# A two-layer streaming encoder on one core: attention of each chunk worked between the dense products of the next, and the group map folded into the input weights

## The chip, the core and the metric

The kernel runs on one core of one Trainium2 chip. TensorE (PE in the profile, PEld for its weight loads) multiplies, VectorE (DVE), ScalarE (ACT) and GpSimd (POOL) do the elementwise work, and SyncE (SP) issues nearly all transfers; ACT issues a few. The metric is the device time of one execution in microseconds (us), as the median of several runs.

## The reference

Two layers over a sequence of 2048 tokens of 1024 channels. Everything is float32; the kernel splits each operand into a high part of reduced precision (fp32r) and the remainder, and works a product as three matmuls (high by high, high by low, low by high).

```python
# layer 0
h = rms_norm(x, a_norm)
u, z = split(h @ a_w_in)                       # 1024 -> 1024 + 1024
# four groups of 256 channels, windows 2, 4, 8, 16
pooled = trailing_mean(u, window_of_group) - u  # in time, per channel
mixed = einsum('bsgc,gcd->bsgd', pooled, a_w_group) * a_scale
x = x + (mixed * silu(z)) @ a_w_out
x = x + (p[0] @ ple_w[0]) * sigmoid(x @ ple_gate_w[0])
# shared keys and values, 16 heads of 64
k, v = split(rms_norm(x, kv_norm) @ w_kv);  k = rms_norm_per_head(k)
# layer 1
q, z = split(rms_norm(x, b_norm) @ b_w_in); q = rms_norm_per_head(q)
# strictly causal stick-breaking attention:
#   a[t,s] = sigmoid(l[t,s]) * prod_{s<j<t} (1 - sigmoid(l[t,j]))
o = attention(q, k, v)
x = x + (o * silu(z)) @ b_w_out
x = x + (p[1] @ ple_w[1]) * sigmoid(x @ ple_gate_w[1])
```

## The kernel before, in words

The sequence is worked in four chunks of 512 tokens (`NSUB`, `W5`). Activations lie with channels on the partitions, eight tiles of 128x512 to a chunk; weights are the stationary operand, or the moving one where tokens are wanted on the partitions (`run_kvq`).

The program has two parts, one after the other. The first runs, chunk by chunk, a list of 22 steps (`STEPS`): input products u and z by groups of 256 channels (`run_u`, `run_z`), the pooling sums on DVE and POOL, the group map (`run_m`, four matmul blocks to a chunk), output projection (`run_o`), gate (`run_g`), and q, k and v (`run_kvq`). `load_w` brings the weights of the next step while one runs: either raw, to be split by ACT and by DVE or POOL, or ready split from DRAM (`split_once`). The input x and p come with tokens on the partitions and are turned by TensorE transposes against `ident` (L205, L306). What the second part needs goes to DRAM: q, k, v, the split stream (`x2p`), the stream (`x2d`), and split weights for it (`keep`).

The second part is attention from the last chunk to the first. A slot is one head of one query chunk against one key chunk; it has four iterations. An iteration holds a `front` (two matmuls for logits, sigmoid on ACT, the running product as a scan on DVE), a `turn` of an older slot (four transposes, then a copy on ACT and a subtraction on DVE that split the weights) and a `gather` (two matmuls with v). `LAG_T` and `LAG_G` are how many iterations later than its front a turn and a gather stand. Between them a generator (`filler`) yields dense matmuls at a fixed rate: the z products while chunk 3 is in attention (`gate_z`), and the closing products of chunk c+1 (`post`) while chunk c is. The closing products of chunk 0 follow alone at the end, and results are turned by transposes (L765) before they are stored.

Within each engine instructions run in their order; the building layer sets that order by its own estimate of when operands are there. All transfers on SP stand in one queue, and each waits there until its buffer is free.

Of the kernel before, what the change touches and what calls it, by code (L numbers as in the profile page):

```python
# [20 lines left out]
PLE = 256  # L21
W5 = 512
NSUB = S // W5
EPS = 1e-6
WIN = (2, 4, 8, 16)
STEPS = 22
HALO = 16

# [6 lines left out]
def trunk_kernel(ctx, tc, x, p, a_norm, a_w_in, a_w_group, a_scale, a_w_out, kv_norm, w_kv,  # L35
                 k_norm, b_norm, b_w_in, b_q_norm, b_w_out, ple_w, ple_gate_w, out):
# [6 lines left out]

# [3 lines left out]
    V.memset(ones, 1.0)  # L47
    neghalf = cp.tile([P, 8], F32, name="neghalf")
# [10 lines left out]
    r2all = cp.tile([P, NSUB, 4], F32, name="r2all")  # L59
    r2s = [r2all[:, s, :] for s in range(NSUB)]  # L60


    x2d = [[dram.tile([P, W5], F32, name=f"x2d{s}_{o}") for o in range(KT)] for s in range(NSUB)]
    x2p = [[dram.tile([P, 2, W5], F32, name=f"x2p{s}_{o}") for o in range(KT)] for s in range(NSUB - 1)]
    zd = [[dram.tile([P, W5], F32, name=f"zd{s}_{o}") for o in range(KT)] for s in range(NSUB)]
    qd = [[dram.tile([P, 2, W5], F32, name=f"qd{s}_{m}") for m in range(NH // 2)] for s in range(NSUB)]
    kd = [[dram.tile([P, 2, W5], F32, name=f"kd{s}_{m}") for m in range(NH // 2)] for s in range(NSUB)]
    vd = [[dram.tile([8, P, 4, P], F32, name=f"vd{s}_{b}") for b in range(2)] for s in range(NSUB)]
    ve = [[dram.tile([4, W5], F32, name=f"ve{s}_{b}") for b in range(2)] for s in range(NSUB)]

    wod = [dram.tile([P, 2, 2, 4, P], F32, name=f"wod{o}") for o in range(KT)]
    wgd = [dram.tile([P, 2, 2, 4, P], F32, name=f"wgd{o}") for o in range(KT)]
    wzd = [dram.tile([P, 2, 2, 4, P], F32, name=f"wzd{o}") for o in range(KT)]
    wld = [dram.tile([P, 2, 2, P], F32, name=f"wld{o}") for o in range(KT)]

    def rsqrt_mean(out_ap, ss, n, pool, tag):
# [3 lines left out]
        G.tensor_tensor(out=out_ap, in0=ms, in1=neghalf[:, 0:w], op=ALU.pow)  # L80

    state = {"w": 0, "first": True, "deep": False}
    split_once = {}

    def load_w(pools, src, kts, c0, n, gain=None, kept=None):


        wraw, wpair = pools
        units = []
        srcr = src.rearrange("(k q) n -> q k n", q=P)  # L90
        kk = min(W5 // n, kts)
        for k0 in range(0, kts, kk):
            pr = wpair.tile([P, 2, kk, n], F32R, tag="wpair", name="wpair")
            units.append(pr)
            if (kept, c0, k0) in split_once:
                nc.sync.dma_start(out=f(pr), in_=split_once[kept, c0, k0])
                continue
            if state["deep"]:
                raw = io.tile([P, kk, n], F32, tag="io", name="wraw")
            else:  # L100
                raw = wraw.tile([P, kk, n], F32, tag="wraw", name="wraw")
            (nc.scalar if state["first"] else nc.sync).dma_start(out=raw, in_=srcr[:, k0 : k0 + kk, c0 : c0 + n])
            if gain is None:
                A.copy(out=pr[:, 0], in_=raw)  # L104
                state["w"] += 1
                (G if state["w"] % 3 else V).tensor_tensor(out=pr[:, 1], in0=raw, in1=f(pr[:, 0]), op=ALU.subtract)  # L106
            else:
                for j in range(kk):
                    g = gain[:, k0 + j : k0 + j + 1]
                    A.activation(out=pr[:, 0, j], in_=raw[:, j], func=AF.Identity, scale=g)  # L110
                    V.scalar_tensor_tensor(out=pr[:, 1, j], in0=raw[:, j], scalar=g, in1=f(pr[:, 0, j]),  # L111
                                           op0=ALU.mult, op1=ALU.subtract)
            if kept is not None:
                d = split_once[kept, c0, k0] = dram.tile([P, 2, kk, n], F32, name=f"{kept}_{c0}_{k0}")
                nc.sync.dma_start(out=d, in_=f(pr))
        return units

    def wst(units, kt, hl, c0, n=P):
        kk = units[0].shape[2]
        return units[kt // kk][:, hl, kt % kk, c0 : c0 + n]  # L120

    def product(pss_, units, acts, c0s, order=None):

        order = order or range(len(acts))
        for kt in order:
            for ps, c0 in zip(pss_, c0s):
                T.matmul(ps, wst(units, kt, 0, c0), acts[kt][:, 0], start=(kt == order[0]), stop=False)  # L127
                T.matmul(ps, wst(units, kt, 0, c0), acts[kt][:, 1], start=False, stop=False)  # L128
                T.matmul(ps, wst(units, kt, 1, c0), acts[kt][:, 0], start=False, stop=(kt == order[-1]))  # L129
# [748 lines left out]
```

## Time and profile before

| what | value |
|---|---|
| median of 3 runs | 2831.4 us (2830.37 to 2831.97) |
| span of the profiled execution, first to last instruction | 2822.5 us |
| PE busy | 2747.1 us (97%) |
| DVE, ACT, POOL busy | 1892.6, 1409.9, 953.8 us |
| transfers | 576.43 MB, 204 GB/s in the mean |

The profile is of one execution, of which the span is known and no separate time; the median of the runs lies 8.9 us above the span, which is what stands around it (start and end of the execution). Busy time of PE is the union of its matmuls, whose ends are modelled; the mean time of one matmul in the groups is longer than the distance between starts, since matmuls overlap, and the distance is what counts.

### The profile page before, as it was taken

Reading aid. Unit: us, or ns where it says so; the run is one execution under the profiler, and the core shown is the slowest. Engines: PE = TensorE matmul, PEld = TensorE weight load, DVE = VectorE, ACT = ScalarE, POOL = GpSimd, SP = SyncE. Lnnn points to the kernel's source line nnn. Section 1 sums busy time; section 2 is a strip of 40 time slices with the busy share of each in tenths; the row PEclk is TensorE's granted clock in tenths of the full one; section 3 lists DMA queues with packets and bytes.
Section 4 is the critical chain, followed back from the end, with each engine's and each line's share of the span. In section 5 each row is a group of like instructions: output and inputs, shape, how many; then the busy total and the mean of one; then the engine's idle time right before and its main releaser. Section 6 shows DMA issues by size and latency. Waiting matters only on the chain. (4 is left out here: it accounts for less than half of the span.)

```text
span 2822.5 us, 40373 instructions
## 1 busy us (share of the span) xinstructions
PE 2747.1 (97%) x13667; PEld 2271.8 (80%) x13667; DVE 1892.6 (67%) x2581; ACT 1409.9 (50%) x2765; POOL 953.8 (34%) x965
## 2 busy tenths in 40 slices
PE   8999999999999999999899999999999999999999
PEld 6788788888888888888778888887878778878877
DVE  6655534555355543445289999999999998886642
ACT  5445523455244542445356555666666665664431
POOL 3564346643475425644211112121211122223220
PEclk9999999999999999999999999999999999999999
DMA  7855695557855678446666565455555565658765
GB/s 270 274 173 205 238 317 166 175 208 246 303 167 176 221 248 285 147 147 203 213 198 218 185 208 177 161 168 183 171 162 171 168 189 183 195 184 262 242 203 160
DMA packets 335139, 576.43 MB, mean 204 GB/s; under 512 B 32782, under 2 KB 161838, under 8 KB 334932
## 3 DMA queue, kind: packets, MB, share of 16 engines
q1 hardware_dynamic: 327944, 564.34, 60.8%
q10 hardware_dynamic: 6988, 9.50, 1.1%
q8 instruction: 108, 1.77, 0.3%
q14 instruction: 99, 0.81, 0.1%
HBM read 433.16 MB, written 132.19 MB: 200 GB/s over the span
## 5 line engine op out<-in xcount | busy, mean ns | idle before, releaser
L356 PE MATMUL psd<-wpair,x 128*128 128x512 f32 x2304 | 544.0, 393 | 0.0
L630 ACT CAST at<-psa 128x512 fp32r<-128x512 f32 (+3 forms) x640 | 333.4, 522 | 404.8 <-PE psa L627 399.9
L613 DVE TENSOR_TENSOR_SCAN pp<-kap,pp,zeros 128x512 f32<-128x512 f32 x384 | 511.7, 1334 | 5.0 <-ACT kap L606 2.8
L356 PEld LDWEIGHTS psd<-wpair,x 128*128 128x128 f32 x2304 | 428.1, 188 | 86.3
L631 DVE TENSOR_TENSOR at<-psa,at 128x512 fp32r<-128x512 f32 (+3 forms) x640 | 379.7, 595 | 59.2 <-ACT at L630 56.5
L627 PE MATMUL psa<-ident,pp 128*128 128x128 f32 x2176 | 347.4, 275 | 25.0 <-DVE at L631 20.4
L606 ACT ACTIVATE kap<-psl 128x512 f32<-128x512 f32 (+3 forms) x640 | 343.9, 538 | 17.0 <-PE psl L603 8.2
L627 PEld LDWEIGHTS psa<-ident,pp 128*128 128x128 f32 x2176 | 263.3, 140 | 102.8 <-DVE at L631 45.7
L608 POOL TENSOR_SCALAR_AFFINE_SELECT kap<-kap 128x128 f32<-128x128 f32 x256 | 91.7, 359 | 626.8 <-ACT kap L606 532.3
L602 PE MATMUL psl<-kk,qa 128*128 128x512 f32 (+3 forms) x640 | 281.3, 440 | 4.2 <-ACT vr L393 3.5
L613 DVE TENSOR_TENSOR_SCAN pp<-kap,zeros 128x128 f32<-128x128 f32 (+3 forms) x256 | 213.9, 836 | 40.5 <-POOL kap L608 37.0
L640 PE MATMUL pso<-at,vv 128*128 128x512 f32 (+3 forms) x640 | 235.4, 368 | 0.0
L603 PE MATMUL psl<-kk,qb 128*128 128x512 f32 (+3 forms) x640 | 234.6, 367 | 0.0
L639 PE MATMUL pso<-at,vv 128*128 128x512 f32 (+3 forms) x640 | 232.5, 363 | 1.3 <-ACT at L630 1.2
L127 PE MATMUL psd<-xp,wpair 128*128 128x512 f32 x512 | 200.2, 391 | 2.4 <-ACT xp L172 2.4
L111 DVE SCALAR_TENSOR_TENSOR wpair<-wraw,gains,wpair 128x512 fp32r<-128x512 f32 x192 | 149.6, 790 | 78.4 <-ACT wpair L110 78.1
L128 PE MATMUL psd<-xp,wpair 128*128 128x512 f32 x512 | 200.1, 391 | 0.0
L129 PE MATMUL psd<-xp,wpair 128*128 128x512 f32 x512 | 199.8, 390 | 0.0
L110 ACT ACTIVATE wpair<-wraw,gains 128x512 fp32r<-128x512 f32 x192 | 136.8, 720 | 113.2 <-DMA wraw<-in_w_kv_dram 69.2
L106 POOL TENSOR_TENSOR wpair<-wraw,wpair 128x512 fp32r<-128x512 f32 x107 | 146.0, 1369 | 62.1 <-ACT wpair L104 40.7
L104 ACT CAST wpair<-wraw 128x512 fp32r<-128x512 f32 x160 | 97.7, 619 | 114.2 <-PE psd L129 109.1
L639 PEld LDWEIGHTS pso<-at,vv 128*128 128x128 f32 x640 | 120.5, 188 | 28.4 <-ACT at L630 2.6
(204 smaller groups left out, 5488.9 us busy)
## 6 DMA issues: line engine op xcount, KB each, us to landing
wpair<-wi SPq DMA_DIRECT2D x96, 512.0 KB
kk<-kd SPq DMA_DIRECT2D x320, 128.0 KB
vv<-vd SPq DMA_DIRECT2D x160, 256.0 KB
wraw<-in_w_kv_dram SPq DMA_DIRECT2D x128, 256.0 KB
wpair<-wzd SPq DMA_DIRECT2D x64, 512.0 KB
wpair<-wod SPq DMA_DIRECT2D x64, 512.0 KB
wpair<-wgd SPq DMA_DIRECT2D x64, 512.0 KB
wi<-wpair SPq DMA_DIRECT2D x32, 512.0 KB
```

What stands on the lines that cost most here:

```text
L127: T.matmul(ps, wst(units, kt, 0, c0), acts[kt][:, 0], start=(kt == order[0]), stop=False)
L128: T.matmul(ps, wst(units, kt, 0, c0), acts[kt][:, 1], start=False, stop=False)
L356: T.matmul(pss2[i], ck["x2"][kt][:, xh, tk], wst(ws, kt, wh, 0, W5), start=(kt == 0 and xh == 0 and wh == 0), stop=(kt == KT - 1 and wh == 1))
L602: T.matmul(ps[:, :w], qa[:, qs], kk[:, :w], start=True, stop=False)
L603: T.matmul(ps[:, :w], qb[:, qs], kk[:, :w], start=False, stop=True)
L606: A.activation(out=kp[:, r0:], in_=ps[:, :w], func=AF.Sigmoid, scale=-1.0)
L613: V.tensor_tensor_scan(out=pp[:, r0:][:, ::-1], data0=kp[:, r0:][:, ::-1], data1=zeros.to_broadcast([P, w]), initial=1.0 if st["diag"] els ...
L627: T.transpose(pt[:, j * P : (j + 1) * P], pp[:, r0 + kt * P : r0 + (kt + 1) * P], ident)
L630: A.copy(out=at[:, 0, cs], in_=pt[:, cs])
L631: V.tensor_tensor(out=at[:, 1, cs], in0=pt[:, cs], in1=f(at[:, 0, cs]), op=ALU.subtract)
L639: T.matmul(po[:, cs], vv[:, kt, :], at[:, 0, cs], start=(st["diag"] and kt == 0), stop=False)
L640: T.matmul(po[:, cs], vv[:, kt, :], at[:, 1, cs], start=False, stop=(st["last"] and kt == 3))
```

## The change

The whole body is written anew; the operations of attention stay as they were. What is different:

- **Order of the work.** There is one stream of dense work for all chunks (`stream`): the first part of a chunk up to its first eight heads' q, k, v (`first_part`), the other eight heads (`second_part`), and so on to chunk 3, then the closing products of chunks 0 to 2 (`post`). Attention now goes from chunk 0 to chunk 3. Only the first part of chunk 0 and the closing products of chunk 3 stand alone. In between, every iteration of attention on chunk c has the dense products of chunk c+1 (for chunk 3: the closing products) before and after its gather, 1584 dense matmuls to the 64(c+1) iterations of a chunk (`rate`).
- **Group map.** Since the pooling acts on time and the map on channels, `fold` multiplies the u columns of the input weights by the group map once (48 matmuls of 256 columns per group), stores the split product, and `run_m` and its 48 matmuls per chunk are gone. Two of the folds stand ahead of the first dense product, two between those of chunk 0.
- **Layouts.** The host lays x, p and the result out by channels and the weights in the blocks that are loaded, so the transposes of x, p and the result are gone. The squares of x for its norm are summed over channels by POOL and by small matmuls with `ones` (L274).
- **Buffers.** Dense products have two PSUM banks beside attention (six while they stand alone); weights have 9 units of 512 KB (`UNITS`), given back one by one (`give_back`) as the last token tile or channel block has used them; raw weights, x and other inputs share six tiles (`io`). Scans run in place. `LAG_T`, `LAG_G` are 5 and 6, before 6 and 8.
- **Engines.** The pooling adds all run on DVE, the splitting of the chunks' x on POOL; the split of gated outputs moves from ACT and DVE to ACT and POOL, goes to DRAM and comes back. In `keyed`, reduction, root and multiplication of a token tile are issued together; before, they were issued for two tiles at a time.

```diff
+    def pump():
+        while wq["out"] < len(plan) and wq["out"] - wq["back"] < UNITS:
+            ...
+            held.append(unit(key, src, kts, n, gain, keep))
+            wq["out"] += 1
...
+    def fold(g):
+        (wg, _), = take(1)
+        ...
+                raw = io("uraw")
+                nc.sync.dma_start(out=raw, in_=wu_t[2 * g + c, :, h * W5 : (h + 1) * W5])
+                ...
+                    for l, r in ((0, 0), (1, 0), (0, 1)):
+                        T.matmul(ps[:, e], parts[c, kt // 4][l][:, ks], wg[:, r, c],
                                 start=(c == 0 and l == r), stop=(c == 1 and r == 1))
+                        yield
+            ...
+            nc.sync.dma_start(out=d, in_=f(pr))
...
+    def keyed(s, kind, b, j, ps, rj):
+        ...
+        V.tensor_reduce(out=ss, in_=sq.rearrange("q (h d) -> q h d", d=HD), op=ALU.add, axis=AX.X)
+        rsqrt_mean(rq, ss, HD, "q")
+        V.tensor_tensor(out=q8, in0=q8, in1=rq.unsqueeze(2).to_broadcast([P, 8, HD]), op=ALU.mult)
...
+    def first_part(s):
+        yield from mixer(s)
+        x1 = yield from out_steps(ck["m"], lambda o: x[o * P : (o + 1) * P, s * W5 : (s + 1) * W5])
+        ple = load_ple(0, s)
+        yield from gate_steps(x1, ple, put_x2(s))
+        ck["side"] = prep(s + 1) if s + 1 < NSUB else iter(())
+        yield from every(gate_z(s), 48, ck["side"])
+        for kind in "qkv":
+            yield from every(kvq(s, kind, 0), 48, ck["side"])
...
+    def stream():
+        yield from first_part(0)
+        for c in range(NSUB):
+            yield from second_part(c)
+            if c < NSUB - 1:
+                yield from first_part(c + 1)
+        for c in range(NSUB - 1):
+            yield from post(c)
...
+    for n in range(4 * len(slots) + LAG_G):
+        ...
+            turn(active[i2], j2)
+        ...
+            front(active[i], j)
+        fill(x_ / 2)
+        ...
+            gather(active[i3], j3)
+        fill(x_ / 2)
+    for _ in run:
+        pass
+    state["solo"] = True
+    for _ in post(NSUB - 1):
+        pass
```

Three places show how the order moves. The first is PE's row in an iteration of attention. Before, with chunk 3 in attention (`psa` are the transposes, `psl` the logits, `pso` the products with v, `psd` the dense products, here the z products of a chunk read back from DRAM, `xz`):

```order
L627 MATMUL psa<-ident,pp 128x128 x4
L602 MATMUL psl<-kk,qa 128x512
L603 MATMUL psl<-kk,qb 128x512
L668 MATMUL psd<-xz,wpair 128x512
L670 MATMUL psd<-xz,wpair 128x512
L672 MATMUL psd<-xz,wpair 128x512
L639 MATMUL pso<-at,vv 128x128
L640 MATMUL pso<-at,vv 128x128
```

And now, with chunk 1 in attention and the q, k, v products of chunk 2 between (L421; the numbered `x` are the eight tiles of its stream):

```order
L646 MATMUL psa<-ident,pp 128x128 x4
L628 MATMUL psl<-kk,qa 128x512
L629 MATMUL psl<-kk,qb 128x512
L421 MATMUL psd<-wpair,x_11005 128x512 x2
L421 MATMUL psd<-wpair,x_11114 128x512 x3
L421 MATMUL psd<-wpair,x_11214 128x512
L658 MATMUL pso<-at,vv 128x512
L659 MATMUL pso<-at,vv 128x512
L421 MATMUL psd<-wpair,x_11214 128x512 x2
L421 MATMUL psd<-wpair,x_11333 128x512 x3
L421 MATMUL psd<-wpair,x_11418 128x512 x2
```

An iteration holds 13 dense matmuls where it held 3, and they are of the earlier stage, whose weights DVE must split.

The second place is DVE's row in the q and k products. Before, in the first part, between the reduction of squares (L422) and the multiplication by the root (L430), where L111 splits weights, and L173 splits the next chunk's x:

```order
L422 TENSOR_REDUCE ssq<-sqq 128x8
L111 SCALAR_TENSOR_TENSOR wpair<-wraw,gains,wpair 128x512
L422 TENSOR_REDUCE ssq<-sqq 128x8
L430 TENSOR_TENSOR qn<-qs,rq 128x512 x2
L111 SCALAR_TENSOR_TENSOR wpair<-wraw,gains,wpair 128x512 x3
L173 TENSOR_TENSOR xp<-pst,xp 128x512
L422 TENSOR_REDUCE ssq<-sqq 128x8
```

Now, late in the program, with attention's scans (L635) and subtractions (L650) around the same pair (L463, L466) and the splitting of weights (L136):

```order
L463 TENSOR_REDUCE ssq<-sqq 128x8
L466 TENSOR_TENSOR qs<-qs,rq 128x512
L650 TENSOR_TENSOR at<-psa,at 128x512
L635 SCALAR_TENSOR_TENSOR pp<-pp,zeros 128x512
L650 TENSOR_TENSOR at<-psa,at 128x512
L635 SCALAR_TENSOR_TENSOR pp<-pp,zeros 128x128
L650 TENSOR_TENSOR at<-psa,at 128x512
L635 SCALAR_TENSOR_TENSOR pp<-pp,zeros 128x256
L136 SCALAR_TENSOR_TENSOR wpair<-wraw,gains,wpair 128x512
L463 TENSOR_REDUCE ssq<-sqq 128x8
L136 SCALAR_TENSOR_TENSOR wpair<-wraw,gains,wpair 128x512
L466 TENSOR_TENSOR qs<-qs,rq 128x512
```

The multiplication, which needs POOL's root, follows its reduction with nothing or one instruction between, and attention's scans now queue behind it.

The third place is SP's queue at the start. Before, x (`xin`) is loaded at once and the first stores of split weights (`wi`) follow it:

```order
L465 DMA grow<-in_a_norm_dram 8x128
L182 DMA xin<-in_x_dram 128x512 x8
L472 DMA hrow<-in_k_norm_dram 1x64 x2
L465 DMA grow<-in_a_scale_dram 8x128
L465 DMA grow<-in_b_norm_dram 8x128
L465 DMA grow<-in_kv_norm_dram 8x128
L472 DMA hrow<-in_b_q_norm_dram 1x64 x2
L115 DMA wi_0_369<-wpair 128x1024
```

Now the group maps and z weights come first, then three of the eight x tiles, the stores of the split z weights (`once`), and only then the u weights for the folds (`uraw`):

```order
L146 DMA wraw<-in_a_w_group_dram 128x512 x2
L146 DMA wraw<-in_wz_a_dram 128x512 x4
L297 DMA xin<-in_x_dram 128x512 x3
L150 DMA once_336<-wpair 128x1024
L150 DMA once_345<-wpair 128x1024
L150 DMA once_354<-wpair 128x1024
L150 DMA once_363<-wpair 128x1024
L237 DMA uraw<-in_wu_t_dram 128x512 x4
L297 DMA xin<-in_x_dram 128x512 x5
L237 DMA uraw<-in_wu_t_dram 128x512 x4
```

The first matmuls of PE, those of the fold, stand behind the u weights, and the u weights behind four stores that wait for ACT and DVE.

More of the change, by code (lines that the diff above doesn't have):

```diff
@@ L118, in wst @@
[L118 to L129, printed above, removed]
@@ new lines, in mixer @@
+    def mixer(s):
+        ck = chunk[s]
+        ck["m"] = {}
+        for g in (3, 2, 1, 0):
+            us, zs = take(4), []
+            for k in range(2):
+                ps = dense()
+                yield from product(ps, us, ck["x"], k * P, k)
+                zs.append(silu(ps, ck["rb1"]))
+            us = take(4)
+            for k in range(2):
+                ps = dense()
+                yield from product(ps, us, ck["x"], k * P, k)
+                pooled(s, 2 * g + k, ps, zs[k])
+            if s == 0 and g > 1:
+                yield from fold(g - 2)
@@ new lines, in trunk_kernel, with fill @@
+    for _ in fold(3):
+        pass
+    side = prep(0)
+    for _ in range(KT):
+        next(side)
+    for _ in fold(2):
+        pass
+    for _ in side:
+        pass
+    until((0, 0))
+    state["solo"] = False
+    begin(0)
+    begin_v(0)
+    for _ in range(24):
+        next(run)
+    owed = 0.0
+    count = 0
+    def fill(share):
+        nonlocal owed, count
+        owed += share
+        while owed >= 1.0:
+            next(run, None)
+            owed -= 1.0
+            count += 1
+            if count % 36 == 0 and kept:
+                keep(*kept.pop(0))
```

1255 lines of the change are left out of this document (563 added, 692 removed).

## The prediction

> **What bounds the kernel now.** I read the table of engines, then what PE waited for, then busy times by stretches cut where the kind of work changes. PE carries the time:
>
> ```profile
> PE 2747.1 (97%) x13667; PEld 2271.8 (80%) x13667; DVE 1892.6 (67%) x2581; ACT 1409.9 (50%) x2765; POOL 953.8 (34%) x965
> ```
>
> Only 75.4 us of the span are not PE's, so a change gains by taking matmuls away, or by at most those 75. The stretches say where they lie (columns: length, then busy us of each engine, granted clock, DMA share, GB/s):
>
> ```profile
> 0.00:20.00 20.00, 8.32 (x27) 5.79 (x28) 7.10 (x53) 11.69 (x30) 1.02 (x8) 1.00 0.72 252
> 20.00:250.00 230.00, 223.38 (x991) 183.43 (x990) 139.42 (x215) 103.18 (x202) 124.87 (x107) 0.99 0.67 229
> 250.00:1250.00 1000.00, 994.78 (x4549) 823.42 (x4548) 488.23 (x692) 433.29 (x776) 493.54 (x428) 1.00 0.64 217
> ...
> 1380.00:1450.00 70.00, 55.92 (x270) 42.94 (x268) 37.40 (x47) 26.77 (x52) 11.19 (x15) 0.93 0.71 214
> 1450.00:2680.00 1230.00, 1202.85 (x6604) 1000.71 (x6603) 1106.27 (x1404) 735.03 (x1524) 256.72 (x341) 1.00 0.60 190
> 2680.00:2822.50 142.50, 131.90 (x630) 107.88 (x628) 49.29 (x78) 38.80 (x82) 21.16 (x25) 0.97 0.57 182
> ```
>
> PE's idle time is 11.7 us at the start, 6.6 in the rest of chunk 0, 5.2 in 1000 us of dense work (0.5%, DVE 49% busy), 14.1 at the joint between the parts, 27.2 in 1230 us of attention (2.2%, DVE 90% busy) and 10.6 in the last 142. In attention PE waits for DVE:
>
> ```profile
> PE psa L627 <- DVE at L631: 20.4, 40, 1.3
> ```
>
> **The change, part by part.** The distance between starts of dense matmuls, in a run of them and beside attention, and of attention's own (start, duration, line):
>
> ```profile
> 1290.70 20.46 PE L356 MATMUL psd<-wpair,x 128*128 128x512 f32 x89
> 1311.00 1.03 PE L439 MATMUL pst<-ident,qn 128*128 128x128 f32 x8
> ```
>
> ```profile
> 1603.65 0.40 PE L668 MATMUL psd<-xz,wpair 128*128 128x512 f32 x1
> ...
> 1604.35 0.39 PE L639 MATMUL pso<-at,vv 128*128 128x512 f32 x1
> ...
> 1604.81 0.60 PE L627 MATMUL psa<-ident,pp 128*128 128x128 f32 x4
> 1605.16 0.47 PE L602 MATMUL psl<-kk,qa 128*128 128x512 f32 x1
> 1605.47 0.39 PE L603 MATMUL psl<-kk,qb 128*128 128x512 f32 x1
> 1605.70 0.39 PE L668 MATMUL psd<-xz,wpair 128*128 128x512 f32 x1
> ...
> 1615.92 0.28 PE L639 MATMUL pso<-at,vv 128*128 128x256 f32 x1
> 1616.04 0.28 PE L640 MATMUL pso<-at,vv 128*128 128x256 f32 x1
> ```
>
> A dense matmul takes 20.30/89 = 0.228 us in a run and 0.70/3 = 0.233 beside attention; one of 256 columns 0.12; four transposes 0.35, and the matmul behind them comes 0.08 late (0.31 for 0.23), so 0.43. One full iteration of attention is 0.46 (v) + 0.43 + 0.47 = 1.36 us of PE.
>
> 1. The group map's 4 x 48 matmuls go: 192 x 0.228 = -44.
> 2. The folds come: 192 of 256 columns x 0.12 = +23.
> 3. Transposes of x (128), p (64) and the result (128) go, 80 groups of four x 0.43 = -34 (0.35 to 0.45 a group: -28 to -36). Their copies on ACT and DVE lay beside PE and count nothing.
> 4. 16 more one-column matmuls for the norm of x, each at most a transpose's 0.09: +2.
> 5. Dense matmuls beside attention are 6336, before 2064 (z products and three of four closings). At 0 to 0.005 us more each the 4272 cost 0 to 21; the runs between are now 6 to 13 long for the first chunks, so nearer the run: +8.
> 6. The joint goes: attention starts while the stream has more to give. 14.1 us idle, and 0.07 of clock over 70 us (4.9): -14 to -19, I take -16.
>
> 7. **The opening.** Ahead of the last u tile of the first fold SP has issued 5.5 MB, of the second 7.9 MB (0.26 MB a raw tile, 0.52 a split one). At the 252 GB/s of the first 20 us that is 22 and 31 us; the first z product follows the second fold at about 34. By then PE has worked some 12 us, so 22 are lost where 11.7 were: +10. The last folded weights of chunk 0 stand 37.2 MB down the queue, and PE comes to them after 22 + 23 + 7 x 48 x 0.228 = 122 us. What the queue delivers:
>
> ```profile
> 60.00:100.00 40.00, 40.00 (x178) 33.14 (x177) 29.52 (x51) 20.68 (x45) 17.86 (x19) 1.00 0.80 278
> 705.60:776.20 70.60, 70.60 (x317) 58.44 (x316) 26.00 (x41) 16.33 (x31) 33.03 (x36) 1.00 0.88 303
> ```
>
> At 303 GB/s 37.2 MB take 123 us, at 278 134, at 252 148: 1 to 26 us late, of which I take 8. Together +18, between +8 and +36. The Trainium skill (DMA: Bandwidth & Descriptors, Specifications) gives about 358 GB/s to a core; the 303 GB/s at a share of 0.88 agree (344 at a full share), and by the page's figure the queue would be done at 104 us, the 8 would fall away and the sum would be 8 lower.
>
> 8. **Stalls beside attention.** Durations of DVE and of POOL's root (POOL is the second fence):
>
> ```profile
> L613 DVE TENSOR_TENSOR_SCAN pp<-kap,pp,zeros 128x512 f32<-128x512 f32 x384 | 511.7, 1334 | 5.0 <-ACT kap L606 2.8
> L631 DVE TENSOR_TENSOR at<-psa,at 128x512 fp32r<-128x512 f32 (+3 forms) x640 | 379.7, 595 | 59.2 <-ACT at L630 56.5
> L613 DVE TENSOR_TENSOR_SCAN pp<-kap,zeros 128x128 f32<-128x128 f32 (+3 forms) x256 | 213.9, 836 | 40.5 <-POOL kap L608 37.0
> L111 DVE SCALAR_TENSOR_TENSOR wpair<-wraw,gains,wpair 128x512 fp32r<-128x512 f32 x192 | 149.6, 790 | 78.4 <-ACT wpair L110 78.1
> L430 DVE TENSOR_TENSOR qn<-qs,rq 128x512 f32<-128x512 f32 x64 | 49.0, 766 | 42.6 <-POOL rq L80 42.3
> L422 DVE TENSOR_REDUCE ssq<-sqq 128x8 f32<-128x512 f32 x64 | 43.7, 682 | 67.8 <-ACT sqq L420 67.8
> L448 DVE SCALAR_TENSOR_TENSOR hl<-pst,gqk,hl 128x512 fp32r<-128x512 f32 x32 | 23.1, 744 | 0.0
> ```
>
> ```profile
> L80 POOL TENSOR_TENSOR rq<-ms,neghalf 128x8 f32<-128x8 f32 x64 | 109.3, 1708 | 5.3
> ```
>
> Attention asks DVE for about 1.33 + 0.67 = 2.0 us a full iteration and 1.3 a diagonal one, PE for 1.36 and 0.9. One block of q or k (96 matmuls, 22.1 us of PE) asks DVE for 8 x 0.79 + 4 x 0.68 + 4 x 0.77 + 4 x 0.74 = 15.1. With 11.3 iterations beside it in chunk 2 that is DVE 35 against PE 36 us, with 15.5 in chunk 3 43.5 against 42. Outside q, k and v DVE has a fifth to spare. And the multiplication behind the reduction now waits for POOL's 1.7 us with nothing or one instruction between, with attention's scans queued behind it. Before, that wait was 42.3/64 = 0.7 us and cost PE nothing; now I put it at 1 to 2, four times a block: +5 us, so 40 against 36 in chunk 2 (four blocks) and 49 against 42 in chunk 3 (two). The lag of turn behind front, about one and a half iterations, swallows some 5 us once in each pair, which leaves 8 + 9 = 17 of stall. The rest: 985 us beside chunks 0 and 1 at 0.5%, 5 us, and about 910 beside 2 and 3 at attention's 2.2%, 20. Together 42, of which 27 were there: +15, between -15 and +60.
>
> 9. The end: the same 432 closing matmuls alone; the last turn and its copy (about 1 us) go, the last pair of gated outputs now takes a split on POOL: 0, between -3 and +6.
>
> Sum: -44 + 23 - 34 + 2 + 8 - 16 + 18 + 15 = -28 on the span of 2822.5, 2794.5; with the 8.9 us by which the median stands above the span, 2803. ACT (50%) stays covered, as does the unchanged volume of transfers (about 580 MB).
>
> **The rivals.**
>
> *Nearly no stalls.* Beside attention DVE's load is now even, and PE loses 0.5 to 1% throughout, as it did at 49%: 15 us in place of 42, and the queue of the opening keeps up: 2803 - 27 - 8 = 2768. For it speaks the dense stretch; against it the 90% stretch, whose load the blocks of q and k reach again. Chance 0.23.
>
> *Transfers hold PE in chunk 0.* Opening at 252 GB/s: 18 later than taken. Beside attention on chunk 0, 121 MB in 456 us are 265 GB/s, and the kept weights, stores and k, q, v share one queue; if six blocks wait 2 us each: 2803 + 18 + 12 = 2833. Against it: 303 GB/s went with PE never idle. Chance 0.14.
>
> *DVE becomes the bound (slower).* The place is q, k and v beside chunks 2 and 3. POOL's work, 21% of attention's stretch before, is about 32% beside chunk 2, and the same operation is longer with the other engine at work, on both:
>
> ```profile
> L173 DVE TENSOR_TENSOR x<-ta,x 128x512 fp32r<-128x512 f32 x32 | 32.2, 1007 | 36.5 <-ACT x L172 35.4
> ...
> L173 DVE TENSOR_TENSOR x<-tx,x 128x512 fp32r<-128x512 f32 x32 | 22.2, 693 | 13.4 <-ACT x L172 13.0
> ```
>
> ```profile
> L265 POOL TENSOR_TENSOR zr<-zr,sg 128x512 f32<-128x512 f32 x32 | 42.5, 1350 | 23.7 <-ACT sg L264 20.2 <-DMA wpair<-wi 3.5
> ...
> L712 POOL TENSOR_TENSOR zr<-zr,sgz 128x512 f32<-128x512 f32 x32 | 63.1, 1971 | 174.4 <-issue 83.5 <-DVE os L645 74.0 <-ACT sgz L711 12.0
> ```
>
> If DVE runs 10% longer there, each of the nine blocks is some 4 us over PE, and POOL's late root adds 1 to 2 us at each of 24 tiles: +50, so 2853. It decides from about 7% on, where 22 us are eaten. Beside this stands the Trainium skill (SBUF — State Buffer, the reading of its diagram): DVE with two SBUF inputs and GpSimd share a port pair under an exclusive lock, and the loser blocks for a whole instruction; the pairs of rows above agree in kind. Chance 0.17.
>
> **How the numbers follow.** My sum has 0.46; 2803 is its time, with 2780 to 2822 its own range. The range of all reaches from 2762 to 2856, which leaves a tenth on either side. Within 0.2% (5.7 us, about what a measurement tells from no change) of 2831.4 lies most of the transfers' case: same 0.10. Slower: the DVE case and some of the transfers', 0.20. Faster: 0.70.
>
> **What would show it.** PE's busy time should fall by about 45 us to some 2700; the first dense product start near 34 us; no gap at any change of chunk over 3 us; PE's waits beside chunks 2 and 3 be for DVE's subtraction, densest in q and k, with DVE itself waiting for POOL's root about 1.5 us each. I am wrong if PE's idle time passes 125 us (then look whether DMA or DVE is named), or if PE's busy time does not fall.

## The result, and the profile after

The changed kernel takes 2964.6 us (median, 2961.81 to 2968.24); the kernel before took 2831.2 beside it. The ratio is 1.0473, 95% interval 1.0459 to 1.0488: 133 us slower, where 28 us faster was forecast. The profiled execution has a span of 2960.0 us. Its table of engines:

```profile
PE 2763.0 (93%) x13376; PEld 2260.2 (76%) x13376; DVE 1955.7 (66%) x2513; ACT 1355.7 (46%) x2642; POOL 966.2 (33%) x961
```

PE's idle time went from 75.4 to 197.0 us (+122), and its busy time did not fall by some 45 but rose by 16. What PE waited for (total, times, longest):

```profile
PE pst L475 <- DVE qs L466: 70.8, 16, 9.7
PE psd L248 <- ACT uh L239: 24.4, 4, 19.3
PE pso L659 <- DVE at L650: 20.3, 29, 2.7
PE psd L221 <- ACT mp L117: 9.8, 4, 4.7
```

L475 is the turn of finished rows of q or k (`finish`), the transposes that lay them out by channels. There are 16 groups of rows, and PE waits at every one: at 15 for the multiplication L466 (at one of them twice), at the last for a copy on ACT (5.4 us). L659 is attention's product with v; it waits for DVE's subtraction about as long as attention's transposes did before (20.4). By stretches (columns as in the prediction):

```profile
0.00:140.00 140.00, 113.53 (x569) 96.75 (x570) 88.86 (x190) 61.68 (x123) 48.57 (x48) 0.98 0.82 284
...
320.00:420.00 100.00, 81.39 (x366) 65.59 (x365) 46.45 (x66) 43.95 (x75) 34.46 (x35) 0.93 0.62 196
420.00:800.00 380.00, 350.99 (x1606) 287.05 (x1606) 204.11 (x263) 158.52 (x318) 189.60 (x190) 0.96 0.79 258
800.00:960.00 160.00, 132.97 (x619) 107.29 (x618) 90.36 (x129) 76.99 (x145) 58.13 (x61) 0.91 0.56 175
960.00:1320.00 360.00, 349.75 (x1704) 288.21 (x1702) 245.60 (x296) 160.76 (x328) 147.52 (x147) 0.99 0.60 188
1320.00:1500.00 180.00, 159.45 (x764) 129.83 (x765) 117.02 (x158) 94.91 (x180) 58.66 (x67) 0.94 0.53 166
...
2160.00:2840.00 680.00, 660.64 (x3392) 540.31 (x3391) 541.13 (x637) 323.14 (x643) 110.66 (x123) 0.99 0.67 210
```

The three bad stretches, 320 to 420, 800 to 960 and 1320 to 1500, are where rows of q and k end. There PE loses 66 of 440 us, and the granted clock is 0.91 to 0.94. DVE is busy 46 to 65% of them, so it is not at its limit. Two of the waits end before attention's first matmul (391.2 us); from 320 to 391 us:

```profile
PE pst L475 <- DVE qs L466: 12.9, 2, 7.5
```

Chunk by chunk the waits are 21.4, 23.3, 15.7 and 10.3 us: they are largest where the least attention runs beside the products. One such wait, from the timeline of all engines (start, duration, engine, line; in brackets the idle time ahead and what ended it):

```profile
806.31 0.67 ACT L459 ACTIVATE qs<-psd,r 128x512 f32<-128x512 f32 x1
...
808.76 0.64 PE L421 MATMUL psd<-wpair,x 128*128 128x512 f32 x2
...
810.71 0.62 ACT L117 CAST xp<-xin 128x512 fp32r<-128x512 f32 x1 [2.56 <-DMA xin<-in_x_dram]
...
811.77 0.61 ACT L461 ACTIVATE sqq<-qs 128x512 f32<-128x512 f32 x1
...
812.41 0.69 DVE L463 TENSOR_REDUCE ssq<-sqq 128x8 f32<-128x512 f32 x1 [1.45 <-ACT sqq L461]
812.63 1.27 POOL L288 TENSOR_TENSOR acc<-acc,sq 128x512 f32<-128x512 f32 x1
...
815.48 1.65 POOL L114 TENSOR_TENSOR rq<-ms,neghalf 128x8 f32<-128x8 f32 x1
817.10 1.26 POOL L118 TENSOR_TENSOR xp<-xin,xp 128x512 fp32r<-128x512 f32 x1
817.16 1.74 DVE L466 TENSOR_TENSOR qs<-qs,rq 128x512 f32<-128x512 f32 x1 [1.76 <-POOL rq L114]
819.05 0.45 PE L475 MATMUL pst<-ident,qs 128*128 128x128 f32 x1 [9.66 <-DVE qs L466]
```

The last token tile's row leaves ACT at 807.0. Its square stands on ACT behind a cast of the next chunk's x, which waits 2.56 us for its transfer; its root comes on POOL behind that x's sum of squares; the multiplication takes 1.74 us where it mostly takes 0.69, beside POOL's split of x (five of the 64 take over 1.7 us, and all five stand beside a POOL instruction). PE has long come to the turn, and everything behind the turn waits. The granted clock around it (third column from the right):

```profile
806.00:810.00 4.00, 2.69 (x11) 1.72 (x11) 4.00 (x7) 1.96 (x4) 0.00 (x0) 1.00 0.38 122
810.00:814.00 4.00, 0.00 (x0) 0.00 (x0) 1.65 (x3) 2.66 (x5) 2.59 (x3) 0.80 0.96 259
814.00:818.00 4.00, 0.00 (x0) 0.00 (x0) 2.06 (x2) 0.00 (x0) 3.83 (x4) 0.50 0.61 164
818.00:822.00 4.00, 2.95 (x10) 2.51 (x11) 2.11 (x3) 1.38 (x2) 0.36 (x1) 0.50 0.04 15
822.00:826.00 4.00, 4.00 (x22) 3.28 (x20) 1.26 (x3) 2.21 (x6) 0.94 (x1) 0.92 0.98 332
```

It falls to half some 3 us into the wait and is still at half 3 us after its end. So a wait costs twice: its own time, and slow matmuls behind it. Over the span the mean clock is 0.975, before 0.996; (1 - clock) x span is 74 and 11 us. Part of that lies in idle time, so it bounds the slow matmuls from above.

The line in the code that made this is not among those that the prediction weighed. In `run_kvq`, now `kvq`, finished rows are turned later, beside products of the next block:

```diff
-                    while j0 == 0 and kt == KT - 1 and lag:     # behind 48 matmuls
+                if kt in (2, 5) and j < 2 and lag:              # the first behind 9 matmuls
                     lag.pop(0)()
```

48 matmuls are 11 us of PE, 9 are 2 us (and a little more with attention between). The chain from a product's end to its finished row takes 5.3 us where nothing stands between (from 313.11 to 318.36, six instructions on ACT, DVE and POOL), and 12.6 in the wait above (806.31 to 818.90).

### The profile page after: what moved, and what is told of

It is laid out like the page before. It is cut to its first block, busy times and chain, and to the rows that moved or that the text cites. A ratio compares the mean times of both kernels' runs of the same rounds, so it can differ in the third digit from the quotient of the medians.

```text
span 2960.0 us, 39525 instructions
## 1 busy us (share of the span) xinstructions
PE 2763.0 (93%) x13376; PEld 2260.2 (76%) x13376; DVE 1955.7 (66%) x2513; ACT 1355.7 (46%) x2642; POOL 966.2 (33%) x961
## 5 line engine op out<-in xcount | busy, mean ns | idle before, releaser
L635 DVE TENSOR_TENSOR_SCAN pp<-pp,zeros 128x512 f32<-128x512 f32 (+3 forms) x640 | 779.2, 1219 | 119.5 <-POOL pp L633 91.4
L421 PE MATMUL psd<-wpair,x 128*128 128x512 f32 x2304 | 623.9, 408 | 2.2 <-DVE wpair L136 1.4
L650 DVE TENSOR_TENSOR at<-psa,at 128x512 fp32r<-128x512 f32 (+3 forms) x640 | 384.9, 603 | 320.1 <-ACT at L649 318.2
L421 PEld LDWEIGHTS psd<-wpair,x 128*128 128x128 f32 x2304 | 437.0, 196 | 89.7 <-DVE wpair L136 4.1
L646 PEld LDWEIGHTS psa<-ident,pp 128*128 128x128 f32 x2176 | 278.4, 142 | 94.4 <-DVE pp L635 8.3
L631 ACT ACTIVATE pp<-psl 128x512 f32<-128x512 f32 (+3 forms) x640 | 343.6, 538 | 10.2 <-PE psl L629 7.2
L221 PE MATMUL psd<-x,wpair 128*128 128x512 f32 x768 | 304.7, 397 | 9.7 <-ACT sg L397 6.1
L223 PE MATMUL psd<-x,wpair 128*128 128x512 f32 x768 | 303.7, 395 | 0.2 <-DVE x L118 0.2
L226 PE MATMUL psd<-x,wpair 128*128 128x512 f32 x768 | 302.9, 394 | 0.0
L633 POOL TENSOR_SCALAR_AFFINE_SELECT pp<-pp 128x128 f32<-128x128 f32 x256 | 89.5, 350 | 554.4 <-ACT pp L631 553.8
L659 PE MATMUL pso<-at,vv 128*128 128x512 f32 (+3 forms) x640 | 239.9, 375 | 20.8 <-DVE at L650 20.3
L136 DVE SCALAR_TENSOR_TENSOR wpair<-wraw,gains,wpair 128x512 fp32r<-128x512 f32 (+1 forms) x224 | 165.9, 782 | 35.0 <-ACT wpair L135 34.5
L221 PEld LDWEIGHTS psd<-x,wpair 128*128 128x128 f32 x768 | 145.7, 190 | 40.4 <-ACT sg L397 7.5
L135 ACT ACTIVATE wpair<-wraw,gains 128x512 fp32r<-128x512 f32 (+1 forms) x224 | 145.7, 688 | 57.4 <-DMA wraw<-in_w_kv_dram 16.9
```

Source lines behind the costliest of these rows:

```text
L221: T.matmul(ps, hi, acts[kt][:, 0], start=(i == 0), stop=False)
L223: T.matmul(ps, hi, acts[kt][:, 1], start=False, stop=False)
L226: T.matmul(ps, lo, acts[kt][:, 0], start=False, stop=(i == n))
L421: T.matmul(ps, ck["x2"][kt][:, xh, tk], u[:, wh, 0], start=(kt == 0 and xh == wh), stop=(kt == KT - 1 and wh == 1))
L631: A.activation(out=pp[:, r0:], in_=ps[:, :w], func=AF.Sigmoid, scale=-1.0)
L635: V.tensor_tensor_scan(out=pp[:, r0:][:, ::-1], data0=pp[:, r0:][:, ::-1], data1=zeros.to_broadcast([P, w]), initial=1.0 if st["diag"] els ...
```

## The experiments

Two theories. *Position*: PE waits because the turn now stands nearer to its rows than their chain is long. *Load*: DVE or POOL (the prediction's rival) have too much to do beside attention, and the turn is only where it shows. All runs, against runs of the kernel before on the same chip; "turn" is PE's wait at the turn for DVE's multiplication:

| kernel | median us | ratio to before [95%] | PE idle | turn | clock |
|---|---|---|---|---|---|
| before | 2828.5 to 2831.2 | 1 | 75.4 | 0 | 0.996 |
| changed | 2964.6 | 1.0473 [1.0459, 1.0488] | 197.0 | 70.8 | 0.975 |
| e3_before_early | 2930.7 | 1.0360 [1.0345, 1.0375] | 137.2 | 68.2 | 0.979 |
| e10_before_early_fill | 2948.4 | 1.0419 [1.0403, 1.0434] | 114.9 | 43.0 | 0.989 |
| e2_warm | 2986.3 | 1.0561 [1.0543, 1.0579] | 169.1 | 50.6 | 0.982 |
| e11_no_row_norm | 2849.9 | 1.0074 [1.0057, 1.0091] | 123.3 | 0 | 0.988 |
| e1_late_turn | 2921.8 | 1.0332 [1.0308, 1.0357] | 167.9 | 44.7 | 0.983 |
| e5_side_off | 2958.3 | 1.0453 [1.0435, 1.0470] | 195.2 | 67.4 | 0.976 |
| e6_late_turn_side_off | 2903.8 | 1.0254 [1.0239, 1.0269] | 156.7 | 30.1 | 0.984 |
| e7_side_in_gate | 2922.1 | 1.0325 [1.0310, 1.0341] | 165.7 | 24.6 | 0.981 |
| e9_cover33 | 2904.0 | 1.0263 [1.0245, 1.0280] | 160.3 | 9.5 | 0.987 |
| e4_u_first | 2970.0 | 1.0497 [1.0482, 1.0513] | 207.9 | 74.2 | 0.972 |
| b1_before_layouts | 2842.0 | 1.0042 [1.0027, 1.0056] | 112.3 | | 0.986 |
| b2_norm_later | 2835.5 | 1.0022 [1.0012, 1.0032] | 99.0 | | 0.988 |
| b4_norm_dve | 2834.8 | 1.0018 [1.0009, 1.0027] | 107.8 | | 0.991 |
| b3_p_out | 2808.6 | 0.9926 [0.9912, 0.9940] | 78.0 | | 0.995 |

**Position alone: the turn moved in the kernel before.**

```diff
-                    while j0 == 0 and kt == KT - 1 and lag:
+                    while j0 == 0 and kt == 1 and lag:
```

> The kernel before, with the turn of a finished group of q or k rows moved ahead: 12 dense matmuls behind the end of its last token tile, where it stood 48 behind. There is no attention beside these products. Theory 'position alone makes the stall': 16 waits of some 3 to 6 us, with the clock falling behind them; 2831 rises by 60 to 120 us. Rival 'only the load of attention makes the chain of that tile long': less than 40 us.

Measured +102 us, with no attention beside these products. PE's waits:

```profile
PE pst L439 <- DVE qn L430: 68.2, 32, 3.9
```

Idle time rose by 62 us and PE's busy time by 41 (2747.1 to 2788.1), though PE does the same work: position is enough, and a microsecond of waiting costs some 0.65 more in clock. The clock behind one of these waits (2.43 us, ended at 1391.23):

```profile
1388.00:1391.00 3.00, 0.80 (x4) 0.33 (x2) 2.31 (x4) 1.40 (x3) 2.29 (x3) 1.00 0.35 100
1391.00:1394.00 3.00, 1.59 (x5) 0.88 (x5) 0.87 (x2) 0.00 (x0) 1.87 (x2) 0.52 0.24 80
1394.00:1397.00 3.00, 3.00 (x11) 2.41 (x11) 1.50 (x2) 1.38 (x2) 0.00 (x0) 0.50 0.15 61
1397.00:1400.00 3.00, 3.00 (x17) 2.66 (x16) 1.04 (x2) 1.38 (x2) 0.00 (x0) 0.85 0.72 288
```

**The chain left out.** In `keyed` of the changed kernel the square, reduction, root and multiplication are gone, so the rows stay unnormed; the turn stays where it is.

> The changed kernel without the norm of the rows of q and k: squares, reduction, root and multiplication of all 64 token tiles are left out, the turn stands where it stood. Theory 'chain and position': the turn then waits for one ACT operation alone, the 70.8 us of waits fall under 12 and the clock comes back: 2850 to 2880 us, no lower than the kernels with the late turn would reach if their turns waited for nothing. Rival 'DVE's and POOL's load is the bound, the turn only shows it': with 92 us of DVE and 109 us of POOL gone, the waits for DVE's subtraction in attention (20.3 us) fall too, and the time goes under 2835.

Measured 2849.9, at the lower edge of what position forecast. The table of engines, and PE's waits in attention and at the turn:

```profile
PE 2727.7 (96%) x13376; PEld 2240.8 (79%) x13376; DVE 1868.9 (66%) x2385; ACT 1320.6 (46%) x2578; POOL 836.7 (29%) x833
```

```profile
PE pso L652 <- DVE at L643: 19.5, 26, 3.2
...
PE pst L468 <- ACT qs L459: 5.5, 6, 1.3
```

DVE has 87 us less and POOL 129, and PE still waits 19.5 us for DVE in attention (L652 here is L659 of the changed kernel). This run takes away the chain and some of the load together, so it can't part the two by its time alone. But the load that went did not shorten the waits in attention, and with all releasers counted PE's waits at the turn fell from 83.3 to 8.3 us, which is the whole of the 74 us of idle time that went. Of the span, 109 us went (2960.0 to 2851.0): these 74, and 35 of PE's busy time. In medians it is 115 us, the price of the chain at this place; it is most of what the changed kernel lost, and without it the kernel is still 0.74% slower than before.

**Cover against length.** Four edits of the changed kernel: the turn later (e1), the next chunk's x in the middle of tiles (e5), both (e6), both with still more cover (e9).

```diff
-                if kt in (2, 5) and j < 2 and lag:
+                if (j, kt) in ((0, 7), (1, 1), (1, 4), (1, 6)) and lag:      # e1, e6, e7
+                if (j, kt) in ((1, 2), (1, 4), (1, 5), (1, 7)) and lag:      # e9
```

```diff
-            if i % n == 0:       # in every(): a step of the next chunk's x
+            if i % n == 12:      # e5, e6, e9
```

> The changed kernel with one thing moved: the turn of a finished group of q or k rows stands at least 21 dense matmuls (some 5 us) behind the end of its last token tile, where it stood 9 (2 us) behind. Theory 'position': PE waits for the chain of that tile (ACT, DVE, POOL, DVE), so the waits of PE's row transposes for DVE's multiplication (16 waits, 70.8 us) fall under 15 us, and the clock beside them comes back (75 us were lost to it in the span, 11 before the change); time falls from 2965 to some 2850 to 2880 us. Rival 'load': DVE, ACT and POOL are behind by their load, so the waits move to other places with the same sum; time falls by less than 20 us.

> The changed kernel with the steps that bring in and split the next chunk's x (ACT and POOL) moved by 12 matmuls: in a block of q, k or v they stood behind the 48th and the 96th matmul, that is right behind the ends of the second and the last token tile, and now behind the 12th and the 60th, in the middle of tiles. Theory 'the chain of the last tile waits on ACT and POOL behind that step': the 16 waits of the row transposes fall from 70.8 to 25 to 40 us, and the time from 2965 by 30 to 60 us. Rival 'the chain is long by itself and the turn stands too near': the waits stay over 60 us, the time within 10 us.

> Both edits: the turn 21 matmuls behind the end of the last token tile, and the steps of the next chunk's x in the middle of tiles. If cover and length of the chain together make the wait, the waits of the row transposes fall under 10 us (44.7 with the late turn alone) and the clock lost beside them goes too: 2860 to 2890 us. If a third thing holds the chain (the weights' split on ACT, which waits there for raw weights), 20 us or more of waits stay and the time is 2900 or more.

> As the kernel with the late turn and the x steps in the middle of tiles, but the first turn stands 33 dense matmuls (7.5 us) behind the end of the last token tile, where it stood 24. The chain there took 10.8 us at its longest and the longest wait was 5.9. If the wait is cover against length of chain, 2 us more of cover take the 12 waits (30.1 us) under 12 us, and with the clock behind them the time falls from 2904 to some 2875 to 2890. If the chain stretches with the cover, because the building layer orders ACT and POOL by what is wanted first, it stays within 8 us of 2904.

None reached its first forecast. The late turn gave 43 us, between the numbers of the two theories; the steps of x alone gave 6, as their rival had it; both together gave 61, the second case's number, and ACT did wait there for raw weights (1.93 us ahead of a square at 322.18). With 33 matmuls of cover the wait for the multiplication is down to 9.5 us, as the first case had it, and the time did not move:

```profile
PE pst L475 <- DVE hl L482: 15.2, 7, 3.2
PE pst L475 <- DVE qs L466: 9.5, 6, 4.0
```

The four turns of a group now stand close together (behind matmuls 33, 39, 42 and 48), and they wait for DVE to have read an earlier turn out of one of the two banks (L482). With all releasers counted, the waits at the turn went only from 37.6 (e6) to 32.7 us. More cover helps, but these four edits won only about half of the chain's price (61 us of 115). In the kernel before the four turns stand together behind 48 matmuls, and wait 5.1 us for banks that attention does not share; a place as late as that was not tried in the changed kernel, so whether it would win the rest stays open.

**The steps of x taken out of these blocks altogether** (into the gate products, `every(gate_z(s), 18, ...)`; the turn as in e1):

> The late turn, and all ten steps of the next chunk's x moved out of the q, k and v blocks into the gate products ahead of them. Nothing of the next chunk then stands on ACT, POOL or the transfer queue beside the rows. The waits of the row transposes fall under 10 us as with both edits; if the transfers of x held ACT by holding the raw weights in the queue, this one has fewer waits than the kernel with the steps in the middle of tiles. 2855 to 2890 us. Against it: the gate products then carry ten splits, and waits for ACT's sigmoid there could rise from 6 us by some 10.

```profile
PE pst L475 <- DVE qs L466: 24.6, 12, 3.8
PE psd L248 <- ACT uh L239: 23.9, 3, 19.1
PE pst L274 <- POOL acc L288: 20.0, 3, 10.9
```

Measured 2922.1, which misses the forecast. The turn waits less than in e1, which has it at the same place (24.6 against 44.7), so x does lengthen the chain. But the norm's small matmuls (L274) now stand right behind POOL's sum of squares and wait 20.0 us: the same fault at another place.

**Filling the waits.** 18 useless matmuls ahead of the first turn of each group, in the changed kernel and in the kernel before with the early turn:

```diff
+                if m == 0:
+                    x0 = chunk[s]["x2"][0][:, 0]
+                    for i in range(18):
+                        T.matmul(pt.rearrange("q j t -> q (j t)"), x0[:, 0:P], x0, start=True, stop=True)
```

> The changed kernel with 18 useless 512-column matmuls ahead of the first transposes of each of the 16 finished groups of rows, written to the bank that the transposes then overwrite: 16 x 18 x 0.228 = 66 us more of PE work, which stands where PE otherwise waits. Theory 'idle time costs twice, since the granted clock falls behind a wait of several us': PE's idle time falls by some 45 us or more, the mean clock rises, and the time falls by 20 to 45 us though PE does more work. Rival 'the clock falls for other reasons than the waits': the time stays or rises by up to 20 us.

> The kernel before with the early turn, and 18 useless 512-column matmuls (4.1 us) ahead of each of its 16 first turns, written to the bank that the turn then overwrites. The early turn alone cost 102 us: 62 more of idle time, 41 more of busy time at a clock that fell. The useless work is 16 x 18 x 0.228 = 66 us and fits the waits. Theory 'the clock falls because PE waits': with the waits filled the clock stays at 1.00 and the time falls by 30 to 40 us, to some 2890 to 2900. Rival 'the clock falls for another reason, or the filling itself costs': 2925 or more.

Both were slower, by 22 and 18 us, so the gain that both theories forecast did not come. The useless work (66 us) took away only 28 and 22 us of idle time, since the turns still waited behind it. The mean clock did rise with less waiting (0.975 to 0.982, 0.979 to 0.989): in e10 the waits left at the turn are at most 2.2 us, and the stretches with rows ran at 0.98 and 0.99, against 0.96 and 0.95 with the waits unfilled (250 to 1250 and 1250 to 1480).

```profile
PE pst L443 <- DVE qn L430: 43.0, 26, 2.2
```

```profile
250.00:1250.00 1000.00, 963.81 (x4332) 794.38 (x4331) 443.73 (x632) 393.16 (x700) 435.94 (x384) 0.98 0.61 205
1250.00:1480.00 230.00, 221.66 (x1005) 182.54 (x1004) 108.99 (x150) 98.35 (x164) 101.93 (x84) 0.99 0.47 156
```

**The opening.** In `fold`, the raw u tiles asked for ahead of the group weights' units (`take(1)` moved behind the loads):

> The changed kernel with the raw u tiles of a fold asked for ahead of the group weights' units instead of behind them. Theory 'order of the queue': the first fold product starts some 8 us sooner than 19.3 us, and the time falls by 8 to 13 us. Rival 'volume of the queue': the opening needs all that stands in it, and the time stays within 4 us.

```profile
PE psd L248 <- ACT uh L238: 23.9, 1, 23.9
PE psd L248 <- ACT wpair L129: 9.3, 1, 9.3
```

The first fold product did start 10 us sooner (9.28), but PE then waited 23.9 us for the second fold, and the time did not fall (5 us more, with intervals that overlap). The transfers of the second fold's u tiles, in the changed kernel and in e4, say why:

```profile
19.25 3.37 SPq L237 DMA_DIRECT2D uraw<-in_wu_t_dram  x4
...
34.41 1.99 SPq L236 DMA_DIRECT2D uraw<-in_wu_t_dram  x4
```

With the edit they were issued 15 us later, behind stores of the first fold's results (`wf`), for which the queue waits until DVE has made them, and behind loads of these same results. So it is again the order of the queue that held PE; what its volume alone would cost this run does not show.

**The part of the change that takes work away, in the kernel before.** b1 has the three layouts, b2 moves the norm's small matmuls into the middle of the first u product, b4 also sums the squares on DVE, b3 has the layouts of p and the result alone.

```diff
-                    T.transpose(pt[:, j, :], xs[j][o // 4][:, o % 4 * P : (o % 4 + 1) * P], ident)     # b1, b2, b4
-                    T.transpose(pt[:, j, :], pin[j // 2][:, j % 2, k * P : (k + 1) * P], ident)        # all
-                        T.transpose(pt[:, j, :], sg[:, j * P : (j + 1) * P], ident)                    # all
+                T.matmul(ps[:, 0, j : j + 1], acc[:, j * P : (j + 1) * P], ones,                       # b1, b2, b4
+                         start=True, stop=True)
```

> The kernel before with one part of the change alone: the host lays x, p and the result out by channels, the 320 transposes of x, p and the result are gone, and the squares of x are summed over channels by POOL and 16 one-column matmuls. By the prediction's terms: 80 groups of transposes x 0.43 = -34 and +2, that is 2831 - 32 = 2799 us, if nothing waits in their place; between 2795 and 2805. Rival 'the transposes stood in gaps that stay': less than 15 us gained.

```profile
PE pst L212 <- POOL accx L201: 31.4, 4, 10.1
```

Slower by 0.42%, where a gain was forecast: the transposes went, but PE's idle time rose by 37 us, and the largest new wait (31.4 us in four pieces) is at the norm's matmuls, which stand behind POOL's sums.

> The kernel before with the host's layouts of x, p and the result, and the small matmuls for the norm of x moved from the end of the q, k, v blocks, where PE waited 31.4 us in 4 waits for POOL's sum of squares, into the middle of the first u product of the chunk, some 9 us later. If the transposes' 34 us were gained there and were eaten by these waits and the clock behind them (mean clock 0.986 against 0.996), the waits fall under 6 us and the time from 2842 to between 2790 and 2805, faster than both kernels. If PE's busy time had fallen for other reasons than the transposes, 2820 or more.

```profile
PE pst L165 <- POOL rx L80: 17.7, 3, 6.5
...
PE pst L212 <- POOL accx L203: 3.4, 3, 1.4
```

The wait for the sum fell to 3.4 and came back as 17.7 at the next step, the root: still 0.22% slower, and the forecast missed again.

> The kernel before with the host's layouts of x, p and the result, the norm's small matmuls in the middle of the first u product, and the sum of squares on DVE in place of POOL (28 adds, some 0.7 us each, DVE is 49% busy there). If the waits for POOL's sum and root (3.4 and 17.7 us) came from POOL's queue, they fall under 8 us and the clock behind them comes back: 2805 to 2818. If the root's chain waits for ACT or for POOL all the same, 2830 or more.

2834.8, 0.18% slower. The wait for the root rose to 23.0 us (longest 9.0). This run also has the small matmuls earlier in the u product, behind 12 of its matmuls and not 24, so the root's chain had 2.7 us more of products over it and still came later. POOL's adds were thus not what made it long. In the wait that ends at 738.16 the small matmuls are done at 720.85, and the chain's next step, ACT's copy of their sums (L215), starts 12.6 us later:

```profile
732.30 1.28 ACT L508 ACTIVATE kpair<-kraw,gains 128x128 fp32r<-128x128 f32 x4 [4.00 <-DMA vs<-vr]
...
733.49 0.14 ACT L215 COPY ss<-pst 128x4 f32<-128x4 f32 x1
```

It stands on ACT behind work that waits for the transfers of the rows of v (`vs`), and POOL waits 8.30 us for these too. So the same fault shows again: the chain is short, but its queue is not. No run takes those transfers out of the way. None of the three places tried for the norm of x by channels was free of waits.

> The kernel before with the host's layout for p and the result alone; x stays with tokens on the partitions and is turned and normed as before. 64 transposes of p and 128 of the result go, 48 groups x 0.43 = -21 us, and no sum over channels comes. If the transposes' term of the prediction is right where nothing waits in their place, 2828 to 2831 becomes 2807 to 2813; if a group is worth no more than 0.35, 2812 to 2815. Rival 'they stood in gaps, above all the result's, which had waits of their own (6.2 us)': 2818 or more.

```profile
PE 2727.6 (97%) x13475; PEld 2255.8 (80%) x13475; DVE 1894.7 (68%) x2581; ACT 1391.1 (50%) x2733; POOL 958.6 (34%) x965
```

2808.6 against 2829.5 (medians): 0.74% faster (0.60 to 0.88%), 21 us for 48 groups, 0.44 each, as forecast. PE's busy time fell by 19.5 and its idle time rose by 3. This version beats both kernels.

## Why the prediction was wrong

**Terms 1 to 6, the work on PE: right as far as tested.** Transposes are worth 0.44 a group (0.43 taken). The six terms, without the joint's idle time, come to -50 (of it 5 of clock). In the kernel without the chain PE's busy time is 19 lower than before, while (1 - clock) x span is 23 higher (34 against 11), which leaves some -42 of work, against -45 in the sum. The joint's gap went.

**Term 7, the opening: right in its sum.** PE loses 31 us in the first 320 (26.5 to 140, 4.6 after); 18.3 were lost in the first 250 before. +13 measured, +18 taken. The part ahead of the first product was as taken (23.3 us lost, 22 taken), though that product began at 41.4 us, not 34: the two folds ahead of it had waits between them. The 8 us for folded weights that come late are not seen (7.8 us lost from 41.3 to 320, 6.6 before in the rest of chunk 0).

**Term 8, the stalls: this step failed.** It took 42 us of idle time beside attention; from 320 to 2840 us there were 157 (143 of them beside attention, from 391 on), and the slower clock cost up to 63 more over the whole span. The prediction did see that the multiplication now waits for POOL's root, 1 to 2 us each; it measured 127.4/64 = 2.0:

```profile
L466 DVE TENSOR_TENSOR qs<-qs,rq 128x512 f32<-128x512 f32 x64 | 50.7, 792 | 127.4 <-POOL rq L114 127.4
```

But it asked only what is queued behind that multiplication on DVE (the scans), and priced 17 us through DVE's load. It did not ask who on another engine waits for it: the turn, which had moved from 48 to 9 matmuls behind. In the kernel before PE does not wait there for the multiplication at all; the only row of the turn is a short one for its bank:

```profile
PE pst L439 <- DVE hl L448: 5.1, 3, 2.6
```

That is not because the chain was short but because 11 us of products stood over it. That cover went, and what lay under it was charged 16 times.

The rest of term 8 was also too small. Without the chain there are still 46 us of idle time from 320 to 1320, where 5 were taken at 0.5%; most of it (28) lies between 420 and 800, where the mixer, output and gate products follow each other beside attention with two PSUM banks, six before. That the banks are the cause was not tried.

**Term 9, the end: right** (8.6 us of idle time in the last 120, before 10.6 in 142).

**The rivals.** *DVE becomes the bound* had the side, and the place in part (q, k and v, but it named chunks 2 and 3, which have 26.0 of the 70.8 us), not the mechanism; taking 87 us from DVE left attention's waits for it where they were. (Its +50 follows from six blocks of q and k, as in term 8, not from the nine that it names.) The trace after bears out one part of it: the multiplication takes 1.74 us beside POOL's split, against a mean of 0.79. *Transfers hold PE in chunk 0* is not seen: PE's waits for weights that come ready from DRAM are 3.8 us in all; transfers do hold ACT in the chain (2.56 us in the wait shown above). *Nearly no stalls* was wrong.

**The signs named.** PE's idle time passed 125, DVE was named, and PE's busy time did not fall. The gaps at changes of chunk kept to the 3 us allowed (2.24 at the longest); larger ones, up to 4.7 us, stand at changes of product within a chunk (`mp`). Nothing in the prediction allowed for the clock: it took the joint's 0.07 as a gain, and did not carry it to the waits that it forecast.

**The 8.9 us added at the end.** They are not what stands around an execution: where a run has both numbers, its time lies about 2 us above its span (2961.81 and 2960.0 in the changed kernel). The profiled execution of the kernel before was thus some 7 us faster than its median. Differences of idle and busy time against that one profile can be off by as much; the readings that carry the argument (62, 71 and 74 us) are much larger.

## What to carry to other kernels

When a step that consumes a chain of other engines is moved nearer to its producer on an in-order engine, price the whole chain, with all that may stand in each queue on its way, against the work that is left between; a wait of zero in the trace before says how much cover there was, not how long the chain is. In these kernels the slow matmuls behind such waits added half to two thirds of the idle time again (35 on 74 us here, 41 on 62 in the kernel before). Parts of a change that only take work away can be tried alone: here one of them was worth 0.74% and was lost in the rest.

## What the runs showed of the hardware

The granted clock halves behind short waits, and sooner than I had thought. In the kernel before with the early turn a wait of 2.43 us, ended at 1391.23, was followed by a clock of 0.52 and 0.50 for 6 us; a second wait of 1.17 us falls into these. The Trainium skill (TensorE: Matmul & The Clock Gate, HAM oscillation — how this bites in real kernels) asks for no idle gaps of PE over some 3.4 us. The waits of 7.5 to 9.7 us agree, this one is shorter.

The length of a wait alone does not decide. In e10 the turn has 15 waits of 2.17 us; at nine of them the clock went to half, at six it did not. Two of them stand in the same order of work, each behind one of 0.77 us; the stretches right behind them are 328.5 to 332 and 703.5 to 707:

```profile
327.32 0.76 PE L443 MATMUL pst<-ident,qn 128*128 128x128 f32 x5 [2.17 <-DVE qn L430]
...
702.48 0.77 PE L443 MATMUL pst<-ident,qn 128*128 128x128 f32 x5 [2.17 <-DVE qn L430]
```

```profile
328.50:332.00 3.50, 3.50 (x14) 2.91 (x13) 1.78 (x3) 0.97 (x3) 0.00 (x0) 0.51 0.63 253
703.50:707.00 3.50, 3.50 (x21) 2.84 (x21) 1.94 (x3) 1.11 (x3) 0.00 (x0) 1.00 0.57 233
```

By the clock's records in the trace, eight of the nine stretches at half clock last 3.41 us, the ninth twice that. So the clock seems to be set anew at steps of 3.41 us, and where a wait falls between two steps may decide. That is inferred from these lengths; no run moves a wait on purpose.
